# A two-layer decoder trunk on one core: the expert gate matrix staged by 48 tokens in two buffers, its loads grouped by four chunks, and one shared ring of split weights

## The chip, the cores and the metric

The kernel runs on one core of a Trainium2 chip. A core has TensorE (PE in the profile, with its weight loads as PEld), VectorE (DVE), ScalarE (ACT), GpSimd (POOL) and SyncE (SP), and 16 DMA engines that all queues share. The metric is the device time of one execution in microseconds (us), as the median of several runs.

## The reference, cut to what matters

Two layers; the change lies in the second half of each, the PEER experts. For every token, 8 heads pick 16 experts each out of 16384, by a top-k over sums of two key scores; the output is a gated sum over the picked experts' rows.

```
def peer_block(hb):                      # 128 tokens
    q = (hb @ wq).reshape(128, 8, 2, 128)
    s = einsum('thpd,hpnd->thpn', q, keys)
    ...                                  # top 16 of each half, top 16 of the 256 sums
    gate = softmax(top_v)                # per token and head, 16 experts: idx, gate
    act = gelu(einsum('thkd,td->thk', u_tab[idx], hb))
    return einsum('thk,thkd->td', gate * act, v_tab[idx])
```

with 512 tokens, D = 1024 and 16384 = 128 x 128 experts.

## The kernel before

The 16384 experts are taken as 128 **chunks** of 128. Tokens 0 to 383 are done densely: for each chunk the kernel multiplies u with all 384 tokens, applies gelu, writes the result A to DRAM (`sA`), and later reads it back, multiplies it by the gate matrix W (128 experts x 384 tokens, mostly zeros) and multiplies with v. Tokens 384 to 511 are done sparsely by gathers. All matmuls on activations run three times, on a high and a low part of both operands (`hi`, `lo`), so each chunk of u or v is 24 matmuls on PE.

`peer` runs in two stages in each layer.

- **The U stage.** `dense_U` (line 793) loads a chunk of u (`raw`, line 102, SP's queue), splits it into `whi` on ACT (L114) and `wlo` on DVE (L116), multiplies (L132 to L134), applies gelu (L798) and writes A (L799, ACT's queue). Between the chunks `build` (line 907) makes W: one call takes 4 tokens, makes one-hot matrices P and Q on DVE (L921, L923, L927 twice), multiplies them on PE (L933 and L934, 8 small matmuls into PSUM tile `pa`), and ACT copies the result into the staging tile `stg` (L935). `stg` holds SG = 96 tokens, 128 x 128 x 96 floats, in one buffer; when it is full, four DMAs on ACT's queue write it to `sW` in DRAM (L939). That makes 96 calls and 4 writes of `stg` in each layer. The gather steps of the sparse tokens run beside it: an indirect DMA from POOL (L957, 512 KB, three buffers) and a reduction on DVE (L967 for u, L978 into `gacc` for v).
- **The V stage.** `spilled` (line 1053) loads and splits a chunk of v, loads A (L1056) and calls `gated` (line 1022): every WG = 2 chunks one DMA loads their W for all 384 tokens (L1026, SP's queue, two buffers); DVE multiplies A by W (L1028), ACT and DVE split it into `gh` and `gl` (L1030, L1032). PE runs 24 matmuls (L1041 to L1043), accumulating into all eight PSUM banks. In layer 0, `next_layer` prepares tables of layer 1 beside it, on DVE, ACT and POOL.

The splits of v have buffers of their own (`vhi`, `vlo`, VB = 3, in the pool `vp` that lives only in the V stage); those of every other weight share `whi`, `wlo` (HB = 3, in the pool `stp` that lives through the kernel). The pool `vp` takes memory that the U stage's pool `rp`, with `stg` in it, has given back, so its first tiles wait until `stg` has been written out.

The order on each engine is set at build time by a list scheduler that simulates the kernel; an engine then runs its instructions strictly in that order, and so does each DMA queue issue its DMAs. `load_split` is put ahead of its place by a priority (line 108). Below, a **unit** is 48 tokens of W, 12 calls of `build`; there are 8 in each layer. The trace is cut where PE ends the 12th call of each unit.

Of the kernel before, what the change touches and what calls it, by code (L numbers as in the profile page):

```python
# [4 lines left out]
F32 = mybir.dt.float32  # L5
# [17 lines left out]
VB = 3  # L23
# [3 lines left out]
UB = 2  # L27
HPN = 500
TD = 384
SG = 96  # L30
WG = 2
GB = 3
HALVES = (slice(0, T // 2), slice(T // 2, T))
EPS = 1e-6
# [7 lines left out]
def trunk(tc, a, dbg=None, layers=L, n_i2=128):  # L42
# [4 lines left out]
    def nm(s):  # L47
        uid[0] += 1
        return f"{s}{uid[0]}"
# [10 lines left out]
    def ptile(shape, tag):  # L60
        return psp.tile(shape, F32, tag=tag, name=nm(tag), bufs=PB[tag])
# [45 lines left out]
    def load_split(src, pool=stp, tags=("whi", "wlo"), bufs=HB):  # L107
        with tc.high_priority(offset=ahead[0]):
            return load_split_(src, pool, tags, bufs)

    def load_split_(src, pool, tags, bufs):
        raw = load_raw(src)
        hi = pool.tile([128, D], F32R, tag=tags[0], name=nm("whi"), bufs=bufs)
        S.activation(hi, raw, AF.Copy)  # L114
        lo = pool.tile([128, D], F32R, tag=tags[1], name=nm("wlo"), bufs=bufs)
        V.tensor_tensor(lo, raw, hi[:].bitcast(F32), op=OP.subtract)  # L116
        return hi, lo
# [674 lines left out]
    sA = [drp.tile([128, 128, TD], F32, name=f"sA{l}") for l in range(L)]  # L792
    sW = [drp.tile([TD // SG, 128, 128, SG], F32, name=f"sW{l}") for l in range(L)]

# [24 lines left out]
    def peer(l, h, rows, gp):  # L819
        pctx = ExitStack()  # L820
        rp = pctx.enter_context(tc.tile_pool(name=f"rp{l}", bufs=2))
# [83 lines left out]
        stg = {}  # L905

        def build(tb, sel, g8):
            st, gh = sel
            NT = 4
            c = slice(NT * g8, NT * g8 + NT)  # L910
            t0 = 128 * tb + NT * g8
            n, o = divmod(t0, SG)
            if o == 0:
                stg[0] = rp.tile([128, 128, SG], F32, tag="stg", name=nm("stg"), bufs=1)
            sh = [128, 128, NT]

            def row(t):
                return t[:, None, :].to_broadcast(sh)

            P_ = rp.tile(sh, F16, tag="P", name=nm("P"))  # L920
            V.tensor_tensor(P_, io4, row(st[:, 0, c]), op=OP.is_equal)  # L921
            Q_ = rp.tile(sh, F16, tag="Qo", name=nm("Qo"))
            V.tensor_tensor(Q_, io4, row(st[:, 1, c]), op=OP.is_equal)  # L923
            Qs = []
            for i in range(2):
                q = rp.tile(sh, F16, tag=f"Q{i}", name=nm("Q"))
                V.tensor_tensor(q, Q_, row(gh[:, i, c]), op=OP.mult)  # L927
                Qs.append(q)
            for b in range(NT // 4):
                ps = ptile([128, 4, 128], "pa")  # L930
                for k in range(4):
                    t = 4 * b + k
                    TE.matmul(ps[:, k], P_[:, :, t], Qs[0][:, :, t], start=True, stop=False)  # L933
                    TE.matmul(ps[:, k], P_[:, :, t], Qs[1][:, :, t], start=False, stop=True)  # L934
                S.activation(stg[0][:, :, o + 4 * b:o + 4 * b + 4], ps[:].rearrange("p t i -> p i t"), AF.Copy,  # L935
                             scale=1.0 / GATE)
            if o + NT == SG:
                for q in range(0, 128, 32):
                    nc.scalar.dma_start(sW[l][n, :, q:q + 32], stg[0][:, q:q + 32])  # L939
# [63 lines left out]
        for tb in range(NB - 1):  # L1003
            sel = select(tb)
            for g8 in range(32):
                build(tb, sel, g8)
                if g8 % 2:
                    more(1)
                    gsteps(1)
# [8 lines left out]
        vp = vctx.enter_context(tc.tile_pool(name=f"vp{l}", bufs=2))  # L1018
# [3 lines left out]
        def gated(i, A):  # L1022
            k = i % WG
            if k == 0:
                wt[0] = vp.tile([128, TD // SG, WG, SG], F32, tag="W", name=nm("W"), bufs=2)
                nc.sync.dma_start(wt[0], sW[l][:, :, i:i + WG].rearrange("n p i t -> p n i t"))  # L1026
            Av = A[:].rearrange("p (n t) -> p n t", t=SG)
            V.tensor_tensor(Av, Av, wt[0][:, :, k], op=OP.mult)  # L1028
            gh = vp.tile([128, TD], F32R, tag="gh", name=nm("gh"), bufs=4)
            S.activation(gh, A, AF.Copy)  # L1030
            gl = vp.tile([128, TD], F32R, tag="gl", name=nm("gl"), bufs=4)
            V.tensor_tensor(gl, A, gh[:].bitcast(F32), op=OP.subtract)  # L1032
            return gh, gl

        def wv(i):
            return load_split(a["v"][l, i], vp, ("vhi", "vlo"), VB)

        def vmm(ps, d, w, g, first, last):
            c = slice(128 * d, 128 * d + 128)
# [13 lines left out]
        def spilled(i):  # L1053
            w = wv(i)
            A = vp.tile([128, TD], F32, tag="A", name=nm("A"), bufs=3)
            nc.sync.dma_start(A, sA[l][i])  # L1056
            return w, gated(i, A)
# [162 lines left out]
```

## Time and profile before

| | us |
|---|---|
| median of 3 runs | 4042.06 (4036.05 to 4042.52) |
| the profiled execution, its own time | 4039.49 |
| its span in the profile | 4037.7 |
| PE busy in the span | 3736.0 (93%) |
| DVE busy | 3271.9 (81%) |
| ACT busy | 1574.4 (39%) |
| mean granted share of TensorE's clock | 0.959 |

In time order the span holds layer 0's mixer and key scores (to about 725 us), its U stage (to 1458.6), its V stage (to about 2070), then the same for layer 1 (U stage to 3481.7, V stage to the end, about 4030). The page's busy shares are means over these stages. The granted clock is 1.00 (2.4 GHz) or 0.50 (1.2 GHz), and a window over both shows a mean.

### The profile page before, as it was taken

The numbers are of one execution on the slowest core, as the hardware profiler recorded it, in microseconds if no ns is written. First come the engines' busy times: TensorE is split into PE (matmuls) and PEld (weight loads), VectorE is DVE, ScalarE is ACT, GpSimd is POOL, SyncE is SP. The second block draws the span as 40 slices with busy tenths as digits, with TensorE's granted clock in tenths as the row PEclk, the third lists the DMA queues.
The fourth block names the chain that finished last, engine by engine and source line by source line (L and its number), as shares of the span: only waits on it lengthen the run. The fifth ranks groups of instructions, "written<-read, shape, count | busy, mean of one in ns | idle before, by whom it ended". The sixth has DMA issues, their size and how long they took to land.

```text
span 4037.7 us, 62842 instructions
## 1 busy us (share of the span) xinstructions
PE 3736.0 (93%) x21878; PEld 3495.3 (87%) x21878; DVE 3271.9 (81%) x9052; ACT 1574.4 (39%) x2510; POOL 903.1 (22%) x1139
## 2 busy tenths in 40 slices
PE   6999999999999766889999999999999997599998
PEld 5888878999898656889988888789998986599998
DVE  6998777999898779997657776779998987678854
ACT  3555533334343223335433445343343432233332
POOL 7444100033232434330000000000232324333300
PEclk9999999999999878999999999999999997799999
DMA  5222462489898899998843335624888887999974
GB/s 197 69 69 74 136 216 86 138 315 312 305 304 293 278 342 335 370 345 284 272 141 120 114 117 170 209 86 142 306 304 318 301 311 273 336 340 342 341 232 144
DMA packets 367631, 947.57 MB, mean 235 GB/s; under 512 B 36609, under 2 KB 188225, under 8 KB 361169
## 3 DMA queue, kind: packets, MB, share of 16 engines
q1 hardware_dynamic: 251168, 572.74, 42.4%
q0 software_dynamic: 73952, 268.56, 19.4%
q10 hardware_dynamic: 42192, 102.25, 6.5%
q8 instruction: 172, 2.82, 0.3%
q14 instruction: 147, 1.20, 0.1%
HBM read 814.44 MB, written 128.97 MB: 234 GB/s over the span
## 4 chain that ended last, share of the span: by engine, by line
PE 70%; DVE 13%; DMA 11%; ACT 2%; issue 2%; POOL 2%; ACTq 0%; SPq 0%; DVEq 0%
PE mm L133 11%; PE mm L132 11%; PE mm L134 11%; DMA sW<-stg 4%; PE mm L1042 3%; PE mm L1041 3%; PE mm L1043 3%; DVE wlo L116 2%; PE pa L1043 2%; PE pa L1042 2%; PE pa L1041 2%; PE pb L1041 2%; PE pb L1042 2%; PE pb L1043 2%; DVE gacc L978 2%
## 5 line engine op out<-in xcount | busy, mean ns | idle before, releaser
L114 ACT ACTIVATE whi<-raw 128x1024 fp32r<-128x1024 f32 x688 | 728.0, 1060 | 1366.9 <-PE mm L133 774.4
L133 PE MATMUL mm<-alo,whi 128*128 128x384 f32 (+1 forms) x3360 | 1216.0, 362 | 14.0 <-DVE alo L123 13.9
L134 PE MATMUL mm<-ahi,wlo 128*128 128x384 f32 (+1 forms) x3360 | 1215.8, 363 | 9.6 <-DVE wlo L116 9.5
L132 PE MATMUL mm<-ahi,whi 128*128 128x384 f32 (+1 forms) x3360 | 1218.0, 364 | 4.3 <-ACT ahi L229 3.5
L116 DVE TENSOR_TENSOR wlo<-raw,whi 128x1024 fp32r<-128x1024 f32 x688 | 839.8, 1222 | 266.4 <-ACT whi L114 262.9
L133 PEld LDWEIGHTS mm<-alo,whi 128*128 128x128 f32 x3360 | 638.3, 190 | 64.2 <-DVE alo L123 15.6
L134 PEld LDWEIGHTS mm<-ahi,wlo 128*128 128x128 f32 x3360 | 638.2, 190 | 60.6 <-DVE wlo L116 12.1
L132 PEld LDWEIGHTS mm<-ahi,whi 128*128 128x128 f32 x3360 | 639.0, 190 | 53.4 <-ACT ahi L229 4.3
L957 POOL DMA_INDIRECT gr<-ur,idi x256 | 282.2, 1102 | 1403.6 <-DVE jk L876 626.7
L957 POOL DMA_INDIRECT gr<-v,idi x256 | 377.8, 1476 | 625.8 <-DVE gacc L978 503.6
L978 DVE SCALAR_TENSOR_TENSOR gacc<-gr,gate,gacc 128x1024 f32<-128x1024 f32 x254 | 324.4, 1277 | 43.1 <-DMA gr<-v,idi 42.7
L1041 PE MATMUL mm<-gh,whi 128*128 128x384 f32 x768 | 230.7, 342 | 122.4 <-ACT gh L1030 46.0
L967 DVE SCALAR_TENSOR_TENSOR gr<-gr,rows 128x1024 f32<-128x1024 f32 x256 | 310.3, 1215 | 17.1 <-DMA gr<-ur,idi 16.8
L933 PE MATMUL pa<-Q,P 128*128 128x128 f16 x768 | 199.1, 296 | 92.9 <-DVE Q L927 46.1
L1042 PE MATMUL mm<-gl,whi 128*128 128x384 f32 x768 | 258.6, 338 | 2.9 <-DVE gl L1032 2.9
L1043 PE MATMUL mm<-gh,wlo 128*128 128x384 f32 x768 | 253.4, 336 | 1.3 <-DVE wlo L116 1.3
L1041 PEld LDWEIGHTS mm<-gh,whi 128*128 128x128 f32 x768 | 143.0, 191 | 126.7 <-ACT gh L1030 82.0
L935 ACT ACTIVATE stg<-pa 128x512 f32<-128x512 f32 x192 | 114.1, 598 | 343.8 <-PE pa L934 253.7
L876 DVE SCALAR_TENSOR_TENSOR jk<-iof,tf,ci 128x50 f32<-128x50 f32 x1024 | 223.5, 262 | 0.0
L1030 ACT ACTIVATE gh<-A 128x384 fp32r<-128x384 f32 x256 | 131.3, 518 | 220.7 <-DVE A L1028 189.9
L934 PE MATMUL pa<-Q,P 128*128 128x128 f16 x768 | 188.3, 295 | 1.4
L927 DVE TENSOR_TENSOR Q<-Qo,gh 128x512 f16<-128x512 f16 x384 | 147.7, 419 | 48.7 <-PE pa L933 48.5
(410 smaller groups left out, 6556.4 us busy)
## 6 DMA issues: line engine op xcount, KB each, us to landing
raw<-u SPq DMA_DIRECT2D x256, 512.0 KB, 5.3
raw<-v SPq DMA_DIRECT2D x256, 512.0 KB, 5.2
raw<-win SPq DMA_DIRECT2D x112, 512.0 KB, 3.7
ada<-ada SPq DMA_DIRECT2D x96, 512.0 KB, 4.7
sA<-uo ACTq DMA_DIRECT2D x256, 192.0 KB, 4.5
sW<-stg ACTq DMA_DIRECT2D x32, 1536.0 KB, 13.9
A<-sA SPq DMA_DIRECT2D x256, 192.0 KB, 5.1
W<-sW SPq DMA_DIRECT2D x128, 384.0 KB, 5.6
```

The costliest lines, as they stand in the source:

```text
L114: S.activation(hi, raw, AF.Copy)
L116: V.tensor_tensor(lo, raw, hi[:].bitcast(F32), op=OP.subtract)
L132: TE.matmul(ps, hi[:, w], ah, start=(j == 0), stop=False)
L133: TE.matmul(ps, hi[:, w], al, start=False, stop=False)
L134: TE.matmul(ps, lo[:, w], ah, start=False, stop=(j == J - 1))
L876: V.scalar_tensor_tensor(jk, iof[:, 0:NCAND], tf[:, hh, k:k + 1], ci[:, hh], op0=OP.is_equal, op1=OP.mult, accum_out=code[:, hh, k:k + 1])
L957: G.indirect_dma_start(out=g[:], out_offset=None, in_=tab, in_offset=bass.IndirectOffsetOnAxis(ap=ids[:, s_:s_ + 1], axis=0))
L967: V.scalar_tensor_tensor(g, g, 1.0, rows, op0=OP.mult, op1=OP.mult, accum_out=dot[:, s_:s_ + 1])
L978: V.scalar_tensor_tensor(acc_, g, gate[:, s_:s_ + 1], acc_, op0=OP.mult, op1=OP.add)
L1041: TE.matmul(ps, w[0][:, c], g[0], start=first, stop=False)
L1042: TE.matmul(ps, w[0][:, c], g[1], start=False, stop=False)
L1043: TE.matmul(ps, w[1][:, c], g[0], start=False, stop=last)
```

## The change

Three sizes and one line: `stg` holds 48 tokens instead of 96 and has two buffers instead of one, so a layer has 8 writes of four DMAs, each DMA of half the size, instead of 4 writes; W is loaded for four chunks at once instead of two (the DRAM layout of `sW` now has blocks of 48 tokens, so the run of contiguous bytes stays 768 B); the splits of v go through the same three buffers `whi`, `wlo` as those of u, and `vhi`, `vlo` are gone.

```
-SG = 96
-WG = 2
+SG = 48
+WG = 4
...
-                stg[0] = rp.tile([128, 128, SG], F32, tag="stg", name=nm("stg"), bufs=1)
+                stg[0] = rp.tile([128, 128, SG], F32, tag="stg", name=nm("stg"), bufs=2)
...
         def wv(i):
-            return load_split(a["v"][l, i], vp, ("vhi", "vlo"), VB)
+            return load_split(a["v"][l, i])
```

The scheduler makes a new order from the U stage on. Three places of it, all in layer 0.

ACT at the end of the U stage. Before, the copies into the last `stg` (`L935`), its write, then the first splits of v and of the gated A:

```order
L935 ACTIVATE stg_11721<-pa_12533 128x128x4
L935 ACTIVATE stg_11721<-pa_12551 128x128x4
L939 DMA sW_121<-stg_11721 128x3072 x4
L114 ACTIVATE whi_15586<-raw_15584 128x1024
L114 ACTIVATE whi_15628<-raw_15626 128x1024
L114 ACTIVATE whi_15988<-raw_15986 128x1024
L1030 ACTIVATE gh_15595<-A_15590 128x384
```

Now, from the end of unit 7 (`stg_11736`) to the end of unit 8 (`stg_12179`), whose other ten copies stand between:

```order
L935 ACTIVATE stg_11736<-pa_12128 128x128x4
L939 DMA sW_121<-stg_11736 128x1536 x4
L935 ACTIVATE stg_12179<-pa_12188 128x128x4
...
L935 ACTIVATE stg_12179<-pa_12571 128x128x4
L939 DMA sW_121<-stg_12179 128x1536 x4
L1030 ACTIVATE gh_15615<-A_15610 128x384
L1030 ACTIVATE gh_15655<-A_15652 128x384
```

Each write has half the elements, the next unit's copies follow a write into another buffer, and the first three splits of v no longer stand behind the last write.

DVE in the last unit, where PE has builds alone (`Qo`, `P`, `Q` are the one-hot matrices of a build, `gacc` the sparse tokens' sum). Before, two builds:

```order
L923 TENSOR_TENSOR Qo_12399<-io_83,slot_11420 128x512
L927 TENSOR_TENSOR Q_12383<-Qo_12381,gh_11422 128x512
L927 TENSOR_TENSOR Q_12385<-Qo_12381,gh_11422 128x512
L921 TENSOR_TENSOR P_12397<-io_83,slot_11420 128x512
L978 SCALAR_TENSOR_TENSOR gacc_6543<-gr_17409,gate_8444,gacc_6543 128x1024
L927 TENSOR_TENSOR Q_12401<-Qo_12399,gh_11422 128x512
L927 TENSOR_TENSOR Q_12403<-Qo_12399,gh_11422 128x512
L923 TENSOR_TENSOR Qo_12454<-io_83,slot_11420 128x512
L921 TENSOR_TENSOR P_12452<-io_83,slot_11420 128x512
L978 SCALAR_TENSOR_TENSOR gacc_6543<-gr_17464,gate_8444,gacc_6543 128x1024
```

Now, in the middle of the same unit:

```order
L923 TENSOR_TENSOR Qo_12401<-io_83,slot_11435 128x512
L921 TENSOR_TENSOR P_12399<-io_83,slot_11435 128x512
L923 TENSOR_TENSOR Qo_12419<-io_83,slot_11435 128x512
L927 TENSOR_TENSOR Q_12403<-Qo_12401,gh_11437 128x512
L927 TENSOR_TENSOR Q_12405<-Qo_12401,gh_11437 128x512
L921 TENSOR_TENSOR P_12417<-io_83,slot_11435 128x512
L927 TENSOR_TENSOR Q_12421<-Qo_12419,gh_11437 128x512
L927 TENSOR_TENSOR Q_12423<-Qo_12419,gh_11437 128x512
```

Some builds have no `gacc` step between them any more; these steps stand later, in the V stage.

SP's queue at the turn from the U to the V stage. Before:

```order
L102 DMA raw_15626<-v 128x1024
L155 DMA ct_15981<-c 128x1024
L102 DMA raw_15986<-v 128x1024
L1056 DMA A_15590<-sA_119 128x384
L1026 DMA W_15592<-sW_121 128x4x192
L1056 DMA A_15632<-sA_119 128x384
```

Now:

```order
L102 DMA raw_15646<-v 128x1024
L155 DMA ct_16001<-c 128x1024
L102 DMA raw_16006<-v 128x1024
L102 DMA raw_16046<-v 128x1024
L102 DMA raw_16086<-v 128x1024
L102 DMA raw_16128<-v 128x1024
L1056 DMA A_15610<-sA_119 128x384
L1026 DMA W_15612<-sW_121 128x8x192
L1056 DMA A_15652<-sA_119 128x384
```

Three more loads of v stand ahead of the first A, and the W load is twice as large.

## Rows read from the trace of the kernel before

**Rows 1.** The page: span, busy time of each engine, the W loads (last: median us to landing).
```profile
span 4037.7 us, 62842 instructions
...
PE 3736.0 (93%) x21878; PEld 3495.3 (87%) x21878; DVE 3271.9 (81%) x9052; ACT 1574.4 (39%) x2510; POOL 903.1 (22%) x1139
...
W<-sW SPq DMA_DIRECT2D x128, 384.0 KB, 5.6
```

**Rows 2.** Waits of the whole run: engine, line, releaser, us in total, times, longest.
```profile
PE pa L933 <- ACT stg L935: 45.0, 6, 9.5
```

**Rows 3.** ACT's timeline at layer 0's first write: start, us, engine, line; idle before, releaser.
```profile
1066.33 4.15 ACTq L939 DMA_DIRECT2D sW<-stg  x4
...
1074.39 1.07 ACT L114 ACTIVATE whi<-raw 128x1024 fp32r<-128x1024 f32 x1 [1.08 <-PE mm L133]
1091.14 1.09 ACT L935 ACTIVATE stg<-pa 128x512 f32<-128x512 f32 x2 [15.69 <-DMA sW<-stg]
```

**Rows 4.** Windows, layer 0: units 2 to 8, then to the first V matmul.
```profile
997.90:1065.70 67.80, 67.80 (x421) 65.33 (x420) 60.12 (x152) 25.87 (x39) 23.41 (x21) 1.00 0.89 304
1065.70:1149.40 83.70, 76.62 (x465) 74.00 (x465) 74.54 (x299) 32.87 (x48) 17.25 (x17) 0.96 0.86 310
1149.40:1214.30 64.90, 64.90 (x402) 61.62 (x402) 59.60 (x150) 24.10 (x37) 21.09 (x20) 1.00 0.91 302
1214.30:1279.00 64.70, 56.42 (x337) 53.26 (x337) 51.90 (x206) 20.99 (x32) 12.68 (x11) 0.89 0.81 289
1279.00:1349.40 70.40, 70.40 (x435) 67.95 (x435) 61.23 (x138) 27.62 (x42) 28.41 (x21) 1.00 0.91 304
1349.40:1395.60 46.20, 31.64 (x197) 27.56 (x196) 28.83 (x58) 10.97 (x19) 15.66 (x9) 0.76 0.76 283
1395.60:1426.20 30.60, 15.38 (x96) 10.15 (x96) 30.60 (x59) 7.18 (x13) 20.32 (x12) 0.50 0.69 208
1426.20:1458.60 32.40, 0.03 (x1) 0.03 (x1) 12.65 (x19) 4.14 (x6) 7.20 (x7) 0.50 0.93 350
```

**Rows 5.** The same in layer 1: units 3, 5, 7, 8, then to V.
```profile
3085.30:3169.80 84.50, 77.81 (x468) 75.44 (x468) 75.04 (x301) 33.02 (x48) 19.42 (x17) 0.94 0.88 315
...
3233.70:3295.90 62.20, 55.72 (x343) 53.64 (x342) 54.70 (x216) 22.30 (x34) 12.33 (x12) 0.95 0.88 316
...
3368.90:3414.00 45.10, 28.33 (x179) 24.27 (x177) 27.61 (x57) 9.77 (x17) 14.06 (x10) 0.74 0.75 282
3414.00:3448.80 34.80, 15.32 (x96) 10.13 (x96) 30.46 (x59) 7.16 (x12) 23.68 (x12) 0.50 0.59 181
3448.80:3481.70 32.90, 0.03 (x1) 0.00 (x0) 12.27 (x13) 4.09 (x6) 8.07 (x8) 0.50 0.94 358
```

The columns of a window are start and end, its length, then busy us and count of PE, PEld, DVE, ACT and POOL, the granted clock, the busy share of the DMA engines and GB/s.

**Rows 6.** DVE's timeline in layer 0's unit 7, columns as in rows 3.
```profile
1387.51 1.28 DVE L978 SCALAR_TENSOR_TENSOR gacc<-gr,gate,gacc 128x1024 f32<-128x1024 f32 x1
1388.70 0.75 DVE L927 TENSOR_TENSOR Q<-Qo,gh 128x512 f16<-128x512 f16 x2
...
1390.05 1.28 DVE L978 SCALAR_TENSOR_TENSOR gacc<-gr,gate,gacc 128x1024 f32<-128x1024 f32 x1
```

**Rows 7.** ACT's timeline after layer 0's last build, columns as in rows 3.
```profile
1426.81 3.75 ACTq L939 DMA_DIRECT2D sW<-stg  x4
1450.52 2.95 ACT L114 ACTIVATE whi<-raw 128x1024 fp32r<-128x1024 f32 x3 [23.73 <-DMA sW<-stg]
```

**Rows 8.** Tile stg: time to landing of its 32 DMAs.
```profile
DMA to landing us min/median/max: 6.9/13.9/23.6
```

**Rows 9.** Windows of the V stages, columns as in rows 4.
```profile
1519.20:1554.20 35.00, 0.05 (x1) 0.05 (x1) 31.75 (x98) 5.59 (x7) 19.43 (x15) 0.56 0.85 284
1554.20:1820.00 265.80, 239.81 (x1321) 234.54 (x1322) 246.70 (x471) 104.59 (x157) 97.02 (x63) 0.96 0.98 359
...
3500.00:4000.00 500.00, 500.00 (x2887) 500.00 (x2886) 360.00 (x443) 185.63 (x242) 103.73 (x78) 1.00 0.89 303
```

**Rows 10.** The chain of waits at the turn from layer 0 to 1: start, us, what.
```profile
2073.10 8.82 DMA pkl<-s5t
```

## The prediction

> **What bounds the kernel now.** PE is busy 93% of the span [rows 1], but that is a mean over stages, so I read stages. The windows of the V stage show its steady part: 2887 matmuls in 500 us, PE never idle, granted clock 1.00 [rows 9]. One 384-column matmul so costs 500/2887 = 0.1732 us, a chunk of 24 of them 4.16 us. The windows of the U stage, cut at units, show that units 2, 4 and 6 are bound by PE in the same way: unit 2 has 421 matmuls, 96 of them the small ones of the builds, so these cost (67.8 - 325 x 0.1732)/96 = 0.12 us, or 11.5 us a unit; with that, unit 4 should take 306 x 0.1732 + 11.5 = 64.5 us and takes 64.9, unit 6 should take 70.2 and takes 70.4 [rows 4]. DVE has 52 to 61 us of work in units 2, 4, 5 and 6: close behind PE, not ahead of it. In units 3 and 5, 7 and 8, PE idles [rows 4, 5].
>
> Who ends that idle time? The list of waits has one line that fits: PE's first matmul of a build waits for ACT's copy into `stg`, six times, 45.0 us in all, the longest 9.5 [rows 2]. ACT's timeline shows why the copy is late: the write of the only `stg` goes out at 1066.3, ACT does another 8 us of work, then stands idle for 15.69 us until the write has landed and copies at 1091.1 [rows 3]. Everything behind that copy in ACT's order (gelu, splits of the next chunks) stands too, and when PE's PSUM tiles are full, PE stops.
>
> The last part of the stage is different. From unit 7's middle PE has builds alone, at half clock (0.50, which is 1.2 GHz), and DVE is busy 30.60 of 30.60 us: it is the bound [rows 4]. DVE's timeline shows the period, 2.54 us from one `gacc` step to the next [rows 6]: 1.20 us for the step and 4 x 0.335 = 1.34 us for a build's four one-hot operations (two of them in 0.75, which overlap by a little). Then PE idles 32.4 and 32.9 us [rows 4, 5]: ACT's next work waits until the last write has landed, 23.73 us [rows 7], and only then v is split and the first A and W are loaded.
>
> **The change, term by term.** The order of the changed program was counted by units; its work is the same, so the durations above hold.
>
> *Two waits per layer in units 3 and 5.* With two buffers of 48 tokens, a copy into a buffer waits for a write issued one whole unit earlier. A unit takes PE at least 50 us until the last two, which take some 27; a write of half the size lands well within that (the slowest whole-size DMA took 23.6, [rows 8]). So these waits go. Worth: units at full clock without a wait against what they took: layer 0, unit 3: 83.7 - (369 x 0.1732 + 11.5) = 8.3; unit 5: 64.7 - 53.2 = 11.5; layer 1: 84.5 - 75.9 = 8.6 and 62.2 - 54.3 = 7.9 [rows 4, 5]. Sum **36.3 us**: about 28 of idle PE, and 8 of matmuls at half clock after it (granted clock 0.89 to 0.96 there, 1.00 in the units beside them). Late next would be DVE: its busy time in units 2 to 6 of layer 0 sums to 307 us, against 343 for PE in the new order, so only in places, not on the whole.
>
> *The end of the U stage.* In the new order unit 7 has 26 large matmuls instead of 101 (layer 1: 81); the rest, 75 and 55, stand earlier, at 0.1732: **+13.0 and +9.5 us**. What is left is DVE's: unit 7 has 12 builds at 1.34, 7 `gacc` steps at 1.20 and 3 splits of v at 1.20 too (operations of the same size), 28 us; unit 8 has 12 builds and 8 steps instead of 12, 25.7, and I take 27, since before 30.5 us of such work took 30.6 and 34.8 [rows 4, 5]. Bounds: 20 a unit if the steps hide behind PE, 35 if the gathers lag as in layer 1.
>
> The last write has half the bytes. Its time is bounded by 6.9 and 23.6 us, the shortest and the longest landing of a whole-size DMA [rows 8]; I take 13, half of the 24 that ACT waited and one more, because the bytes of the gathers beside it do not shrink. After it, an A and a W must land (5.6 us, [rows 1], with the W now twice as large), be multiplied and split: 6.5 instead of 8.1 us (from 1450.5 to 1458.6), since three splits of v no longer stand between (they are done in unit 7 and are in its 28). Together 28 + 27 + 19.5 = 74.5 us, against 109.2 and 112.8 [rows 4, 5]: -34.7 and -38.3, and with the moved matmuls -21.7 and -28.8. Sum **-50.5 us**.
>
> The Trainium skill (DMA: Bandwidth & Descriptors, Anatomy of one DMA) gives each DMA a fixed part of about 2 us beside its bytes at 436 GB/s. By that the last four DMAs, 3.1 MB, would take an estimated 9.2 us, and the sum would be 8 us lower. The trace disagrees for the whole-size write, which took longer than that rule's 16.4 us; so I stay with half of the measured wait.
>
> *The V stage.* In steady state PE is the bound (layer 1, [rows 9]) and the change gives it nothing to do less; the cost of fewer and larger W loads there is nothing, covered by PE's 4.16 us a chunk: a W for four chunks can be asked for four chunks, 16.6 us, ahead. But 14 `gacc` steps per layer that were done in the U stage's end now stand in the V stage, with their gathers of 512 KB. Layer 1 has room (DVE 360 of 500 us). In layer 0 the stretch to 1820 is bound by DMA (share 0.98, 359 GB/s, PE busy 239.81 of 265.8, [rows 9]): 14 x 0.52 MB / 359 GB/s = 20 us more of it, in which PE still does most of its work, since it loses only a tenth of that stretch. Bounds 0 and 20, I take **+4**. Before it, PE stands 35 us (1519 to 1554, [rows 9]), because the three `ada` loads and `c` hold all `raw` buffers until DVE is through layer 1's small tables; the new order has the same 14 loads of v ahead of it and the same 176 small operations, so this stall stays, shifted.
>
> *The turn from layer 0 to 1.* With one ring, the first three weights of layer 1 are split only after the last chunks of v, between the norm's operations; against that the table load, whose 8.82 us now end on the chain [rows 10], is issued before V ends. Bounds: 4 splits' time, 5 us, either way; I take 0.
>
> Sum: -36.3 - 50.5 + 4 = -83 us. The profiled execution took 4039.5 us, 2.6 below the median of the runs, so the forecast is **3957 us** (2% under the median). A measurement here can tell about 0.2% (8 us) from no change.
>
> **Rivals.**
>
> *The DMA engines take it back.* All 14 moved gathers are paid in full in layer 0: 20 instead of 4 us, and if the ramp of V suffers as well, about as much again in layer 1: 3957 + 16 + 16 = **3989**. For it: 0.98 to 1.02 busy share there. Against: layer 1 kept PE at 100 of 100 us. Chance 0.15. The Trainium skill (the same page, Issuing engines are not separate DMA queues) speaks for this one: queues share the 16 engines, and what one queue moves later meets the others' transfers there.
>
> *DVE is the next bound.* Units 3 and 5 lose their wait for `stg`, but PE then waits there for the selection and splits that DVE did meanwhile (74.5 of 83.7 us busy in unit 3, [rows 4]): the first term falls away, **3993**. Against: the new order puts 21 chunks instead of 15 into unit 3. Chance 0.10.
>
> *More is won.* In layer 0's DMA-bound stretch PE idles 26 us [rows 9]; if half as many W loads on SP's queue, and the earlier ones, let A and v come in time, these go: **3931**. Chance 0.15.
>
> *It ends slower.* SP issues in order, and a W load that waits for its buffer holds back every A and v load behind it; twice as large, it also lands later. If every one of the 64 W loads is exposed by half of its 5.6 us [rows 1], that is 179 us: **4136**; it decides from 1.3 us each. Against: 16.6 us of lead. Chance 0.04.
>
> *It does nothing*: the copies still wait, because the second buffer is asked for before the write two units back has landed, and the scheduler's end is as long: **4039**. Against: the unit lengths above. Chance 0.02.
>
> **How the numbers follow.** The forecast has 0.54. The bounds of its own costs (last two units -15 to +28, writes -12 to +16, the turn ±5) make 3930 to 3990, and the rivals at 3931, 3989 and 3993 lie at its ends; I take 3918 to 3998. Faster by over 0.2%: all but the last two, 0.94; no change 0.02; slower 0.04.
>
> **What would show it.** In the new profile the wait of PE for the copy into `stg` is gone from the list, no copy on ACT waits for a write, and PE is idle in no unit from 2 to 6; units 7 and 8 take 26 to 30 us each; the gap before the first V matmul is 17 to 23 us instead of 32. The 35 us stall in layer 0 is there, some 42 us earlier. It would be wrong if units 3 and 5 keep a loss with another releaser (DVE's Q or `wlo`), if the last gap stays near 30, or if layer 0's V stage, 611 us from its first matmul to 2070, grows by more than 10.

## The result, and the profile after

The changed kernel takes **3990.69 us** (median of 4 runs, 3988.25 to 3994.13) against 4039.57 us (4 runs) of the kernel before: a ratio of 0.988 with a 95% interval of 0.9863 to 0.9897, or 49 us less. The forecast was 3957 (83 us less), with a range of 3918 to 3998. So the direction was right, the size two thirds too large; the profiled execution (3988.25 us) shows which steps came as forecast and which did not. The times of kernels below are medians of their runs; one run, of the ring and W for four chunks, took 9418.46 us and is left out.

The page of the changed kernel: span, busy times, W loads (compare [rows 1]).

```profile
span 3986.4 us, 62595 instructions
...
PE 3737.9 (94%) x21878; PEld 3500.6 (88%) x21878; DVE 3270.8 (82%) x9052; ACT 1577.6 (40%) x2510; POOL 883.7 (22%) x1139
...
W<-sW SPq DMA_DIRECT2D x64, 768.0 KB
```

Windows of its layer 0: units 2 to 8, then the gap to the first V matmul (columns as in [rows 4]).

```profile
997.20:1052.70 55.50, 55.43 (x348) 52.69 (x347) 49.72 (x139) 21.39 (x32) 15.97 (x13) 1.00 0.89 322
1052.70:1153.40 100.70, 100.56 (x609) 98.14 (x608) 91.88 (x326) 42.53 (x62) 28.61 (x27) 1.00 0.91 319
1153.40:1207.10 53.70, 53.70 (x338) 50.81 (x337) 47.45 (x135) 21.29 (x33) 14.94 (x13) 1.00 0.89 315
1207.10:1261.20 54.10, 54.10 (x342) 52.03 (x341) 47.16 (x137) 21.48 (x32) 12.17 (x12) 1.00 0.88 309
1261.20:1342.80 81.60, 81.60 (x501) 79.17 (x500) 70.41 (x213) 30.74 (x46) 25.59 (x20) 1.00 0.91 312
1342.80:1367.60 24.80, 17.90 (x123) 14.80 (x122) 24.16 (x52) 9.65 (x16) 9.44 (x6) 0.74 0.85 314
1367.60:1397.10 29.50, 14.15 (x96) 10.52 (x96) 25.59 (x56) 7.19 (x13) 13.81 (x8) 0.50 0.69 242
1397.10:1421.80 24.70, 0.00 (x0) 0.00 (x0) 10.48 (x14) 1.12 (x3) 8.42 (x8) 0.50 0.95 334
```

In units 2 to 6 PE is idle for 0.2 us in all, at full clock. Unit 3 is longer than before because it now holds 21 chunks of u; its 609 matmuls are what it is made of. Units 7 and 8 are bound by DVE (24.16 busy of 24.80, then 25.59 of 29.50; in unit 8 it waits 3.91 us in one piece for a gather to land), and the gap is still there, shorter. None of ACT's copies waits for a write any more, and the wait of PE for the copy into `stg` has shrunk from the 45.0 us of [rows 2] to this, in the list of waits:

```profile
PE pa L933 <- ACT stg L935: 2.3, 4, 0.7
```

The gap itself, ACT's timeline and then SP's and DVE's: the write is issued from 1397.72, its landing lets SP load the first A and W at 1413.15, and W has landed when DVE multiplies at 1420.67. (ACT's row names a load for layer 1's tables, `s5s`, that landed in the same moment; `gh` also needs DVE's product of A and W, which ends there.)

```profile
1397.72 3.65 ACTq L939 DMA_DIRECT2D sW<-stg  x4
1421.27 1.00 ACT L1030 ACTIVATE gh<-A 128x384 fp32r<-128x384 f32 x2 [23.58 <-DMA s5s<-ldt]
```

```profile
1413.15 0.33 SPq L1056 DMA_DIRECT2D A<-sA  x1
1413.52 0.43 SPq L1026 DMA_DIRECT2D W<-sW  x1
```

```profile
1420.67 1.04 DVE L1028 TENSOR_TENSOR A<-A,W 128x384 f32<-128x384 f32 x2 [1.02 <-DMA W<-sW]
```

Windows of layer 0's V stage after the change, cut at the stall and at the last gather step, then layer 1's units 2 to 6, 7, 8, its gap and its whole V stage; below them the two V stages whole, in the kernel before.

```profile
1421.80:1485.40 63.60, 62.95 (x336) 62.15 (x336) 58.20 (x162) 19.94 (x27) 24.79 (x17) 0.94 0.95 335
1485.40:1525.10 39.70, 0.04 (x1) 0.00 (x0) 34.93 (x108) 4.55 (x5) 19.59 (x16) 0.53 0.89 301
1525.10:1841.70 316.60, 283.16 (x1534) 277.12 (x1535) 288.01 (x558) 123.59 (x186) 107.80 (x77) 0.96 0.96 346
1841.70:2059.70 218.00, 217.78 (x1254) 216.58 (x1253) 145.05 (x317) 92.86 (x141) 2.37 (x10) 1.00 0.75 252
3005.40:3350.40 345.00, 344.96 (x2130) 332.67 (x2130) 304.25 (x942) 137.26 (x205) 93.81 (x82) 1.00 0.90 314
3350.40:3375.40 25.00, 17.84 (x123) 14.75 (x121) 24.20 (x52) 9.63 (x16) 9.39 (x6) 0.80 0.82 309
3375.40:3404.90 29.50, 14.15 (x97) 10.49 (x96) 25.55 (x56) 7.18 (x12) 13.82 (x8) 0.50 0.70 243
3404.90:3429.60 24.70, 0.01 (x1) 0.02 (x1) 10.19 (x11) 1.19 (x3) 8.50 (x8) 0.50 0.97 354
3429.60:3969.60 540.00, 540.00 (x3123) 540.00 (x3123) 400.63 (x488) 196.73 (x258) 123.13 (x98) 1.00 0.86 306
```

```profile
1458.60:2071.00 612.40, 551.15 (x3123) 545.05 (x3123) 512.50 (x1128) 240.62 (x360) 140.75 (x103) 0.96 0.89 312
3481.70:4021.80 540.10, 540.07 (x3123) 540.07 (x3123) 383.69 (x472) 196.89 (x258) 110.75 (x84) 1.00 0.86 293
```

Here is what is missing: layer 0's V stage takes 637.9 us instead of 612.4, layer 1's 540.0 as before. Step by step, for both layers together, from the two profiled executions (4039.49 and 3988.25 us):

| step | forecast | measured |
|---|---|---|
| units 2 to 6 (two waits gone, matmuls moved in) | -13.8 | -12.3 |
| units 7 and 8 | -46.7 | -47.9 |
| the two gaps behind the last write | -26.3 | -15.9 |
| V stage of layer 0 | +4 | +25.5 |
| turn from layer 0 to 1, V stage of layer 1 | 0 | -0.9 |
| sum | -83 | -51.5 |

### The profile page after: what moved, and what is told of

Read it like the earlier page. It is cut to its first block, busy times and chain, and to the rows that moved or that the text cites. A ratio compares the mean times of both kernels' runs of the same rounds, so it can differ in the third digit from the quotient of the medians.

```text
span 3986.4 us, 62595 instructions
## 1 busy us (share of the span) xinstructions
PE 3737.9 (94%) x21878; PEld 3500.6 (88%) x21878; DVE 3270.8 (82%) x9052; ACT 1577.6 (40%) x2510; POOL 883.7 (22%) x1139
## 2 busy tenths in 40 slices
DMA packets 371212, 947.55 MB, mean 238 GB/s; under 512 B 36096, under 2 KB 187712, under 8 KB 368848
## 4 chain that ended last, share of the span: by engine, by line
PE 65%; DVE 16%; DMA 11%; issue 4%; ACT 2%; POOL 2%; ACTq 0%; SPq 0%; DVEq 0%; POOLq 0%
PE mm L133 11%; PE mm L132 11%; PE mm L134 11%; DVE wlo L116 3%; DMA gr<-v,idi 3%; PE mm L1042 2%; PE mm L1043 2%; PE mm L1041 2%; DMA gr<-ur,idi 2%; DVE jk L876 2%; DMA ada<-ada 2%; PE pa L1043 2%; PE pa L1042 2%; PE pb L1042 2%; PE pb L1043 2%
## 5 line engine op out<-in xcount | busy, mean ns | idle before, releaser
L957 POOL DMA_INDIRECT gr<-v,idi x256 | 362.2, 1415 | 662.7 <-DVE gacc L978 526.0
L935 ACT ACTIVATE stg<-pa 128x512 f32<-128x512 f32 x192 | 114.4, 598 | 223.3 <-PE pa L934 191.0
L1028 DVE TENSOR_TENSOR A<-A,W 128x384 f32<-128x384 f32 x256 | 139.2, 552 | 57.1 <-DMA A<-sA 52.0
```

The source lines that it names most:

```text
L957: G.indirect_dma_start(out=g[:], out_offset=None, in_=tab, in_offset=bass.IndirectOffsetOnAxis(ap=ids[:, s_:s_ + 1], axis=0))
```

## The experiments

Each kernel was timed against the kernel before on the same chip, whose median there was 4038.8 us for the four parts, 4037.1 for one stage buffer, 4035.3 for the two kernels on the gathers, the 128 bytes and csil early, and 4038.1 for the last three.

### The parts alone

Four kernels take the change apart. W for four chunks has no kernel without the ring: beside `vhi` and `vlo` there is no room for it and the pool of layer 1's tables.

**The stage tile alone**: before, with

```
-SG = 96
+SG = 48
-... tag="stg", name=nm("stg"), bufs=1)
+... tag="stg", name=nm("stg"), bufs=2)
```

> The stage tile alone: 48 tokens in two buffers; W still loaded for two chunks, v still split into buffers of its own. The U stage has the order of the changed kernel, so all theories expect its 28 and 32 us less in the two U stages, and 5 to 8 us less at each gap behind the last write. They part in layer 0's V stage (612.4 us from its first to its last matmul before, 637.9 in the changed kernel). Theory G, the 14 gather steps that now stand in the V stage: it grows by about 25 us here too, total about 3992 us. Theory W, the W load of 768 KB: it grows by under 5 us, total about 3971. Theory R, the ring that u and v share: under 5 us too, about 3971.

Measured 4062.66 us, ratio 1.0057 (1.0043 to 1.0071): slower than before, which no theory had. **The ring alone**: before, with `wv` calling `load_split(a["v"][l, i])`.

> The shared ring alone; the stage tile has 96 tokens in one buffer. The U stage is as before, two gather steps stand later; the gap behind the last write loses the splits of v, 1.6 us a layer. Theory G: V stage of layer 0 within 4 us of 612, total 4035 to 4040 us. Theory W: the same. Theory R: V stage of layer 0 about 20 us longer, total about 4057.

Measured 4045.23 us, ratio 1.0011 (1.0000 to 1.0021); layer 0's V stage 628.6 us, so 16 longer: near the 20 of theory R, against G and W. The total shows 6 of them, not R's 4057, since the gaps and the turn gave some back. **The ring and W for four chunks**, with 96 tokens in one buffer:

> The shared ring and W for four chunks at once; the stage tile has 96 tokens in one buffer, and so two gather steps stand later, not 14. Theory G: V stage of layer 0 within 5 us of 612, the first W of twice the size adds about 1 us at each gap, total 4036 to 4041 us. Theory W: V stage of layer 0 about 20 us longer, total about 4057; by it this kernel is slower than the one with the ring alone, by 15 us or more. Theory R: slower than before, and as the one with the ring alone.

Measured 4057.19 us (five runs, 4049.61 to 4060.80), ratio 1.0044 (1.0029 to 1.0059). In its profiled execution the V stages are as long as with the ring alone (628.3 and 539.5 us), which is theory R; W for four chunks adds nothing to them. But that execution was the fastest of its runs; in the median the kernel is 12 us slower than the ring alone, and its total is the one of theory W. Where these 12 us lie stays open, so theory W is not ruled out. **The change with W for two chunks** (`WG = 2`):

> The changed kernel with W loaded for two chunks instead of four (runs of 384 bytes in DRAM instead of 768). Theory G: V stage of layer 0 about 638 us, total 3988 to 3994. Theory W: it falls back to about 617, total about 3970. Theory R: as G.

Measured 4050.89 us, ratio 1.0031 (1.0021 to 1.0042), 60 us more than with four chunks. No theory had that either. Layer 0's V stage takes 657.0 us in the first and 648.3 in the fourth of these kernels, longer than any theory gave, so these two decide nothing between G, W and R. Layer 1's V stage, which took 540 us before and after the change, takes 596.6 and 595.1 us in them. Their windows of it, and then the first 400 us of that stage in the fourth:

```profile
3443.90:4040.50 596.60, 555.47 (x3123) 547.16 (x3123) 401.67 (x487) 195.64 (x258) 120.20 (x99) 0.98 0.86 279
```

```profile
3436.40:4031.50 595.10, 553.41 (x3122) 544.79 (x3123) 400.88 (x487) 195.34 (x258) 115.66 (x98) 0.99 0.86 279
...
3436.40:3836.40 400.00, 365.46 (x2028) 358.44 (x2029) 287.71 (x341) 129.79 (x169) 100.86 (x87) 0.98 0.93 308
```

The same first 400 us in the changed kernel:

```profile
3429.60:3829.60 400.00, 400.00 (x2297) 400.00 (x2298) 324.50 (x385) 147.45 (x190) 123.13 (x98) 1.00 0.96 347
```

The DMA engines are nearly as busy (0.93 and 0.96) and move 308 instead of 347 GB/s. That is not yet a cause: PE does fewer chunks in these 400 us, and per chunk the bytes are the same (1.46 and 1.45 MB). The lists of waits of this stage in the fourth kernel say what PE waits for, and how little DVE waits for an A or a W:

```profile
PE mm L1041 <- ACT gh L1030: 63.1, 25, 22.9
```

```profile
DVE A L1028 <- DMA A<-sA: 4.7, 8, 1.3
...
DVE A L1028 <- DMA W<-sW: 4.3, 1, 4.3
```

The longest of PE's waits, 22.9 us, lies ahead of its first matmul of the stage; the others come again and again. ACT's timeline at one of them, then PE's first matmul after it:

```profile
3686.75 1.06 ACT L114 ACTIVATE whi<-raw 128x1024 fp32r<-128x1024 f32 x1 [3.10 <-PE pc L1042]
3687.71 0.51 ACT L1030 ACTIVATE gh<-A 128x384 fp32r<-128x384 f32 x1
```

```profile
3688.27 0.79 PE L1041 MATMUL mm<-gh,whi 128*128 128x384 f32 x3 [1.43 <-ACT gh L1030]
```

In ACT's order the `gh` that PE needs next stands behind the split of a later chunk, and that split waits for a buffer of `whi` that PE frees only with its last matmuls. From 3688 to 3901 this comes back every third chunk, 14.2 us apart. In the changed kernel such a `gh` goes ahead of the split that waits for PE:

```profile
3688.18 0.53 ACT L1030 ACTIVATE gh<-A 128x384 fp32r<-128x384 f32 x1 [1.76 <-DVE A L1028]
3689.52 1.06 ACT L114 ACTIVATE whi<-raw 128x1024 fp32r<-128x1024 f32 x1 [0.81 <-PE pc L1042]
```

Followed back through ACT and DVE, 41 of the 41.6 us that PE waits inside the stage end at a split that waits for PE itself, and 0.5 at a load; in the first kernel all of 40.7 us do. So the loss comes from the order on ACT that the scheduler made for these two kernels: 42 us of waits, and 13 us of slower matmuls beside them (553.4 us busy against 540.0). Why it makes this order for 48 tokens and two chunks is not shown; for 96 tokens and two chunks it does not (540.4 us with the ring alone).

The blocks of 48 tokens with two chunks also shorten the run in DRAM to 2 x 48 x 4 = 384 bytes. The page's DMA line, first of the fourth kernel and then of the changed one, has 168192 packets under 512 bytes instead of 36096:

```profile
DMA packets 437774, 947.57 MB, mean 234 GB/s; under 512 B 168192, under 2 KB 254272, under 8 KB 435408
```

```profile
DMA packets 371212, 947.55 MB, mean 238 GB/s; under 512 B 36096, under 2 KB 187712, under 8 KB 368848
```

Over the whole stage the DMA share is 0.86 in this kernel, before and after the change, at 279, 293 and 306 GB/s. The Trainium skill (DMA: Bandwidth & Descriptors, Specifications) names 512 bytes as the smallest transfer at line rate; the lowest of these rates agrees in kind. That the short runs cost this stage any time is not shown. What is shown is that the three sizes stand together: as these kernels are ordered, the smaller stage pays only if W is loaded for four chunks, and that has room only with the ring.

### One stage buffer

The change with `bufs=1` for `stg`.

> The changed kernel with one stage buffer of 48 tokens instead of two, so that each of units 2 to 8 waits for a write of half the size, 14 waits in both layers instead of 6 in the kernel before. Eight gather steps move behind the U stage instead of 14. Theory T, the second buffer removes the waits: a half-size write takes about 14 us, of which 8 us were covered in the waits of before, so PE loses some 3 to 6 us in each of the 10 waits of units 2 to 6 and 10 in each of units 7 and 8: total about 4040 to 4080. Rival, the smaller write does it alone: the copy waits, but PE has enough work in its PSUM tiles, under 1 us each in units 2 to 6: total 3985 to 4025.

Measured 4031.57 us, ratio 0.9985 (0.9972 to 0.9998), 41 us more than with two buffers. The wait is back in its list of waits:

```profile
PE pa L933 <- ACT stg L935: 52.5, 12, 13.1
```

The total lies between the ranges of the two theories, and each holds in its place. Units 2 to 6 take 349 us in either layer against 345.6 and 345.0 with two buffers, and PE's waits for the copy sum to 4.6 and 3.8 us there: PE has other matmuls, and the smaller write does nearly all. Units 7 and 8, where it has none, take 71.0 and 75.8 us against 54.3 and 54.5, with waits for the copy of 19.4 and 24.6 us. (DVE has 8.6 us more work in them as well, 58.3 instead of 49.8: the gather steps that this order does not move.) Their windows in the kernel with one buffer:

```profile
1347.30:1418.30 71.00, 32.26 (x221) 25.57 (x219) 58.33 (x114) 17.03 (x29) 37.32 (x21) 0.58 0.77 268
3371.80:3447.60 75.80, 32.37 (x222) 25.74 (x220) 58.41 (x114) 17.02 (x28) 37.82 (x21) 0.57 0.72 252
```

### The moved gather steps

Two kernels take something from the last 14 gather steps over v in layer 0: one their loads,

```
-g = gather(a["v"].rearrange("l i p d -> (l i p) d"), iv, s_)
+g = gather(...) if l or s_ < 114 else rows
```

> The changed kernel in which the last 14 gather steps over v of layer 0 load nothing: DVE multiplies a tile that is there already (the rows of the tokens) instead of the gathered one. So 14 loads of 512 KB are left out of layer 0's V stage, and DVE does the same work. Of the 25 us by which that stage grew, about 9 are left to the moved gather steps when the ring alone has 16. Theory GD, it is their bytes: the stage falls from 638 to about 625 to 630 us, total 3977 to 3984. Theory GV, it is DVE's 1.2 us each: within 3 us of 638, total 3988 to 3994.

the other their work on DVE (`e = slice(0, D) if l or s_ < 114 else slice(0, 8)` on both operands and the result).

> The changed kernel in which the last 14 gather steps over v of layer 0 are loaded, but DVE adds up only the first 8 of their 1024 columns: 14 times 1.2 us of DVE are left out of layer 0's V stage, the DMA stays. Theory GD, the bytes: within 3 us of 638, total 3988 to 3994 us. Theory GV, DVE's time: the stage falls to 625 to 630 us, total 3977 to 3984.

Measured 3974.50 us (0.9846, 0.9828 to 0.9864) and 3989.55 us (0.9878, 0.9858 to 0.9899). The windows of layer 0's V stage, without the loads and without the work:

```profile
1423.80:2045.80 622.00, 559.94 (x3122) 554.67 (x3123) 526.38 (x1141) 238.89 (x359) 131.37 (x105) 0.95 0.87 306
```

```profile
1424.80:2060.70 635.90, 565.29 (x3122) 559.89 (x3123) 514.68 (x1142) 240.22 (x359) 161.64 (x119) 0.94 0.87 311
```

Without 7.3 MB of loads the stage is 16 us shorter, and the whole kernel too (3990.7 to 3974.5); without the work, which takes 11.7 us from DVE's busy time (526.38 to 514.68), it is 2 us shorter. Theory GD holds against GV, and the loads cost more than the 9 us that it was given, although DVE is busy for 288 of 317 us. With the loads go their bytes, in a stretch with a DMA share of 0.96, and also DVE's waits for gathers to land, 16.2 us in the stage up to its last gather step and 9.0 without the loads; these two were not separated.

### 128 bytes

The change, with this line behind the opening of pool `vp`:

```
+V.memset(vp.tile([128, 32], F32, tag="pad", name=nm("pad"), bufs=1), 0.0)
```

> The changed kernel with a tile of 128 bytes put ahead of the V stage's own tiles in both layers, so that A, W, gh and gl start 128 bytes later; the split weights stay where they were. In the changed kernel and in the two kernels with the ring, a chunk of 24 matmuls takes 4.22 us in layer 0's V stage and 4.16 us in layer 1's; gh starts at an address with the remainder 192 by 256 in layer 0, 64 in layer 1, the weights whi with 64. Theory P, the two starts decide the pace (same remainder 4.16, 128 bytes apart 4.22): here layer 0 takes 4.16 us a chunk and layer 1 takes 4.22, V stage of layer 0 about 630, of layer 1 about 548, total unchanged, 3986 to 3996 us. Theory N, something else in layer 0 slows PE (the tables of the next layer beside it, DMA): layer 0 stays at 4.22 and layer 1 at 4.16.

Measured 3992.53 us, ratio 0.9895 (0.9874 to 0.9916). Windows of the changed kernel in steady parts of the two V stages, then the same windows of the kernel with the 128 bytes, then the first of them in the kernel before:

```profile
1880.00:2040.00 160.00, 159.83 (x909) 159.26 (x908) 107.07 (x230) 66.89 (x101) 1.84 (x7) 1.00 0.75 251
3600.00:3900.00 300.00, 300.00 (x1732) 300.00 (x1732) 229.28 (x280) 112.33 (x146) 67.06 (x55) 1.00 0.91 324
```

```profile
1880.00:2040.00 160.00, 160.00 (x927) 160.00 (x926) 107.78 (x231) 67.59 (x102) 1.84 (x7) 1.00 0.75 256
3600.00:3900.00 300.00, 300.00 (x1707) 300.00 (x1706) 226.38 (x275) 110.26 (x143) 65.73 (x55) 1.00 0.90 319
```

```profile
1880.00:2040.00 160.00, 160.00 (x925) 160.00 (x924) 112.09 (x246) 66.44 (x100) 0.39 (x4) 1.00 0.80 265
```

In layer 0 the matmuls per window rise from 909 to 927, in layer 1 they fall from 1732 to 1707: 1.5% to 2%, the other way round in the two layers, at the same clock. Theory P holds. The kernel before fits it: its splits of v, in buffers of their own, and its `gh` all start with the remainder 192 in layer 0, and it has 925. (The 128 bytes move A, W, `gh` and `gl` together; which of them counts was not tried apart.) Layer 1's V stage grows from 540.0 to 548.7 us; layer 0's falls only from 637.9 to 634.8, as for 420 us of it PE is not the bound.

### The stall, and a smaller stage

**csil early**: `cond` gets a pool of one buffer, opened ahead of that of `s5_small`, and is called there instead of behind the tables.

> The changed kernel with one thing moved: the sigmoid of c for layer 1 (csil) has a buffer of its own ahead of layer 1's small tables, so that it doesn't wait for their memory. Theory S, PE stands 40 us in layer 0's V stage (35 before) because c and three ada loads hold all four raw buffers until csil is written: that stall goes, V stage of layer 0 600 to 612 us, total 3952 to 3965. Rival, DVE and the DMA engines are the bound of that whole stretch: the stall turns up again as waits for W, A and splits until the last gather step, V stage of layer 0 above 625, total above 3977.

Measured **3967.92 us**, ratio 0.9826 (0.9809 to 0.9844). The 40 us stall is gone, but the stage takes 618.5 us, between the two theories. The window from its start to the last gather step:

```profile
1419.60:1860.20 440.60, 388.41 (x2093) 374.04 (x2094) 407.21 (x898) 165.31 (x247) 183.36 (x112) 0.97 0.96 349
```

PE idles 52 us in it: half of the stall has come back, as many short waits for `gh` (32.4 us) and `gl` (18.0). Behind these stands DVE, busy for 407 of the 441 us and waiting 18.9 us for gathers to land, at a DMA share of 0.96. So the rival holds for this half; which of the two engines sets the pace was not separated. **With 128 bytes in layer 0 alone** as well:

> The changed kernel with csil early and the 128 bytes ahead of the V stage's tiles in layer 0 alone. Theory P: both V stages at 4.16 us a chunk. PE is not the bound of the first 440 us of layer 0's V stage, so that only the rest counts: about 43 chunks at 0.06, 3 us less than with csil early alone, total 3961 to 3968. If PE's pace counted over the whole stage it would be 8 us less, 3958 to 3961.

Measured 3968.67 us (0.9825, 0.9809 to 0.9841): no gain over csil early that these runs can tell; the 3 us are not shown. **24 tokens in four buffers, W for eight chunks** (the change with `SG = 24`, `WG = 8`, `bufs=4`), and this with the two edits before:

> The changed kernel with the stage tile halved again: 24 tokens in four buffers, and W loaded for eight chunks at once, so that the runs in DRAM stay 768 bytes. Theory B, the last write's time goes by its bytes (23.7 us for 6.3 MB before, 15.4 us for 3.1 MB in the changed kernel, so about 11 us for 1.6 MB): the gap behind the last build falls from 24.7 to 20 to 21 us in each layer, total about 3982. Rival, the first W, now 1.5 MB, takes it back: it lands 4 us or more later than the 7.1 us of now, the gap stays at 24 to 26, total 3988 to 3996.

> All three together: csil early, 128 bytes in layer 0, 24 tokens in four buffers with W for eight chunks. If they add up: 3968 less 3 less 8, about 3957 us by theory B; by the rival, that the larger first W takes back the shorter write, about 3965.

Measured 4012.51 us (0.9934, 0.9917 to 0.9952) and 4012.01 us (0.9930, 0.9906 to 0.9955). The last write falls to 9.2 us (issued at 1401.09, landed at 1410.25), but the first W, of 1.5 MB, then takes 12.2 instead of 7.1: the gap stays at 23.6 us, close to the 24 to 26 of the rival. With all three together layer 0's V stage takes 635.3 us and not 618.5: what csil early gained is gone there, and why was not followed up. What neither theory had is layer 1's V stage, here without the two edits:

```profile
3432.40:3997.50 565.10, 548.45 (x3123) 544.39 (x3123) 400.24 (x488) 193.30 (x258) 124.25 (x99) 0.99 0.84 290
```

25 us more, 16.7 of them PE waiting. The lists of waits of this stage, first here and then in the changed kernel, say for what, in the main: A lands late.

```profile
DVE A L1028 <- DMA A<-sA: 38.9, 20, 4.7
```

```profile
DVE A L1028 <- DMA A<-sA: 13.6, 12, 2.1
```

SP's timeline in the kernel with 24 tokens, at one W load: it goes out ahead of the next A, whose issue then takes 3.85 us instead of the 0.34 of the one before. DVE, waiting for that A, goes on 15.5 us after its issue:

```profile
3522.62 0.34 SPq L1056 DMA_DIRECT2D A<-sA  x1
...
3527.31 0.38 SPq L1026 DMA_DIRECT2D W<-sW  x1
3527.99 3.85 SPq L1056 DMA_DIRECT2D A<-sA  x1
```

```profile
3543.50 0.56 DVE L1028 TENSOR_TENSOR A<-A,W 128x384 f32<-128x384 f32 x1 [4.73 <-DMA A<-sA]
```

This is one half of the rival that ends slower: a larger W lands later, and the A behind it with it (here W at 3542.95, A at 3543.47). Its other half, a W load that waits for its buffer, is not what acts: SP waits 8.8 us for that in this stage, against 15.2 in the changed kernel. At four chunks neither costs anything (540.0 us). Followed back, some 11 of PE's 16.7 us end at an A, the rest at ACT's order, as in the kernels with W for two chunks.

## Why the prediction was right, and where it was not

**The waits for `stg`.** Right in what it gains: units 2 to 6 came out within 2 us of the sum. The reason given, a second buffer whose write was issued a whole unit earlier, is the smaller part of it there: with one buffer of half the size PE waits 8.4 us for the copies in these units of both layers, against the 36.3 us (28 of them idle) of the prediction's sum. The second buffer pays in units 7 and 8, where with one buffer these waits take 19.4 and 24.6 us. The rival that DVE is the next bound in units 3 and 5 names a time near the measured one, 3993, by a mechanism that is not there: PE is idle for 0.2 us.

**The end of the U stage.** Units 7 and 8 were forecast at 55 us and took 54.3 and 54.5. The step that failed is "I take 13": the write, "half of the 24 that ACT waited and one more", took 15.4 us (1397.72 to 1413.15), and "6.5 instead of 8.1 us" took 8.7, as the larger W needed 7.1 of them; 0.6 us of the last copy stand ahead. A gap is 24.7 instead of 19.5 us, twice. The write was not halved by halving its bytes, and splits that no longer stand in the gap save nothing while the load beside them is longer. The prediction had named 17 to 23 us for this gap.

**The V stage of layer 0.** The step that failed is "Bounds 0 and 20, I take +4": 25.5 us, outside the bounds and past the 10 us that the prediction itself named as a sign of being wrong. The 20 us of DMA work were put beside the idle tenth of PE in that stretch. But the stretch got longer by most of what was added to it: 16 us by the kernel without those loads. PE had to wait more, not less (74.0 us of the stage instead of 61.3), and was busy for 12.8 us more with the same matmuls (563.9 against 551.2). The remaining 9 us are not the gathers: without them the stage still takes 622.0 against 612.4. The pad shows 3 of them, the ring's other addresses; the stall at csil, 35.0 before, is 39.7 in the changed kernel and 38.1 without the loads, 3 to 5 us more, each from one execution; the rest was not separated. The ring had been priced at nothing here, and alone it makes the stage 16 us longer.

**The rivals.** "The DMA engines take it back", at 3989, is where the time came out. Its first half is what happened in layer 0. Its second half, as much again in layer 1, is not: 540.0 against 540.1 us. The two gaps and the ring stand in its place, so that its total fits is luck. The rival that more is won in layer 0's stretch had the sign wrong.

**The range.** It holds the time, 3990.69, because it was taken out past the rivals at 3989 and 3993; by the costs alone it ended at 3990. The costs' own bounds do not follow from the terms: 20 to 35 us for each of four units makes -30 to +30 and not "-15 to +28", the writes' 6.9 to 23.6 us make up to +21 and not +16, and the V stage's up to +16 is not in it.

**W for four chunks** was put down as costing nothing. That holds for layer 1's V stage; in the gaps the larger W is part of the 8.7 us. At two chunks the change would have lost, by ACT's order and not by a price of the loads that these runs show.

## What to carry to other kernels

A size changes the order that a scheduler makes as well as the transfers. Before a loss is put down to the transfers, follow the waits back: what does the waiting engine wait for, and what stands ahead of that on its own engine? Here W for two chunks instead of four brought runs of 384 bytes and turned a gain of 49 us into a loss of 12, and the waits lead to an order on ACT. Where work leaves a stage that is bound by one engine, price it in the stage that it goes to by that stage's own bound: into a stretch with a DMA share of 0.98, moved loads of 7.3 MB came back as 16 us, where 20 had been put down to the bytes and 4 were taken. And a second buffer is worth most where the waiting engine has nothing else to do, which is at the end of a stage, not in its middle.

The best version of this study is the changed kernel with csil early, 3967.92 us: 67 us less than the kernel before on the same chip, and by the two ratios some 22 less than the change.

## What the runs showed of the hardware

In these kernels the pace of a matmul depends on where its operands start in SBUF. With gh and whi at starts whose remainders by 256 are equal, a 384-column matmul takes 0.173 us (1732 in 300 us); with starts 128 bytes apart, 0.176 us (1707 in 300 us), at the same granted clock of 1.00. Moving A, W, `gh` and `gl` together by 128 bytes turned either layer from one to the other. Only these two distances were tried, in this one shape.

A DMA share is not a rate: over layer 1's V stage it is 0.86 in three kernels, at 306 GB/s in the changed one, 293 before and 279 with W in runs of 384 bytes. The first two both have runs of 768 bytes, and what parts them is not shown, so the 384 bytes cannot be given the whole difference.
